# Layer 0's latent columns moved into the context's scan, on one PSUM bank, and the latent scan moved beside the context's selection

## The chip, the cores and the metric

The kernel runs on one core of one Trainium2 chip. The metric is the device time of one execution in microseconds (us). A core has five engines that take their instructions in a fixed order each: TensorE (PE in the profile, its weight loads PEld), VectorE (DVE), ScalarE (ACT), GpSimd (POOL) and SyncE (SP, which here only issues transfers). They wait for each other by semaphores. TensorE writes to PSUM, which holds eight banks of 128 partitions x 512 fp32 numbers.

## The reference

Two layers work on 256 latent tokens `x` and 256 context tokens `z`, 1024 wide; the output is the latents alone. Cut to what matters:

```
def _layer(x, z, c, c_ctx, rows, update_ctx, ...):
    (six modulation vectors of c for x, six of c_ctx for z)
    px = modulate(rmsnorm(x)) @ w_in ;  pz = modulate(rmsnorm(z)) @ w_in
    lat = delta_prep(px) ;  ctx_in = delta_prep(pz)      # conv, SiLU, l2 norm
    oc, sc = gated_delta_chunked(ctx_in, s0=0)           # scan, both directions
    ol, _  = gated_delta_chunked(lat, s0=sc)             # starts from the context's state
    x = x + gate1 * mixer_out(px, ol) @ w_out ;  z likewise   # z only in layer 0
    x = x + gate2 * peer(modulate(rmsnorm(x))) ;  z likewise  # z only in layer 0

def _peer(h, ...):
    scores = (h @ w_query) against sub_keys              # 8 heads, two halves
    idx, gate = top 16 of the pairs of the two halves' top 16
    out = sum_k gate * gelu(h . expert_u[idx]) * expert_v[idx]   # 16384 experts
```

The latents' scan needs the context's scan state, and nothing else of the context. The context's experts (`peer` of `z` in layer 0) need the context's updated `z`, and nothing of the latents.

## The kernel before

The program is written as a list of stages, and a scheduler at build time then decides the order in which each engine's instructions stand; the written order sets its priorities and the order in which shared buffers are handed on. A `Stage` is a piece of SBUF that lives from its opening to its `close()`; a later stage that gets the same addresses waits for the earlier one's last reader. PSUM has names for its eight banks: `pj0`, `pj1`, `c0`, `c1`, `c2`, two of `po`, and one `s`. `bank(shape, tag)` takes the next turn of a name; whoever takes a bank waits until its last user has read it. `using(c0="s", ...)` sends names to other banks for the time of a block: with `c0`, `c1`, `c2` and `pj` all sent to `s`, everything in the block passes through one bank, in the order in which it was written.

The stages of layer 0, by the names used below:

- modulation (L275, vectors 0 to 5 of both token sets): `w_mod` arrives in tiles of 128x1024 (512 KB), four of which fit the ring `w0`, `w1`.
- columns (L404): rmsnorm, transposes into `hT`, then for each part of k, v, q two halves: `columns_by_feature` (16 matmuls 128x128 on 256 columns), copy to `xpad` (L491), convolution on VectorE (L495, L497), SiLU (L500), transposes (L510), for k and q also a norm (L518 to L521) and transposes back (L527). Then `columns_by_token` for the gate `zs` and for the pooling and Fourier heads (L574 to L602).
- scan (L609): four independent chains in the banks `c0`, `c1`, `pj0`, `pj1` (L627 to L680), then steps through `c2`, `c1` into `po` (L704 to L726). Products with the level masks are made on GpSimd (`pool_tt`, L232).
- update (L733): norm of the scan's output, `w_out`, residual.
- select: eight heads of `w_query` and keys on TensorE, top-16 on VectorE. For the context it is `gather_select` (L909), for the latents `dense_select` (L1047) followed by `build` (L1071), which writes a dense gate table to DRAM.
- gather (`gather_rows`, L961): for the context's first 128 tokens `by_choice` fetches 128 rows of `u` and then 128 of `v`, each by one indirect transfer of 512 KB that GpSimd issues (L970) into a ring of seven buffers `uv`. VectorE takes the dot products with u (L982), TensorE sums the v rows (L1005) in bank `s`. For the other 128 tokens `by_token` fetches 128 rows of u and v together.
- stream (L1093): for the latents all 16384 experts, 128 tiles of u and of v; its scores live in bank `s` (L1096), so its first matmul (L1117) waits until `by_choice` has read `s` for the last time (L1010). The gather of `by_token` and layer 1's context run inside it.

Before, the stages are written in this order: context columns, context scan, modulation (2, 4, 3, 5) through `s`, context update, context selection, latent columns, latent scan, latent update, latent selection, build, gather, stream.

Of the kernel before, what the change touches and what calls it, by code (L numbers as in the profile page):

```python
# [24 lines left out]
CTX, LAT = 0, 1  # L25
# [120 lines left out]
def _body(st, tc, a, out, dbg, until):  # L146
# [34 lines left out]
    @contextmanager  # L181
    def using(**kw):
        old = dict(roles)
        roles.update(kw)
        yield
        roles.clear()
        roles.update(old)
# [24 lines left out]
    def dump(key, t):  # L212
        if dbg is not None and key in dbg:
            nc.sync.dma_start(dbg[key], t)

    def to_rows(src, offset, n):
        return bass.AP(tensor=src.tensor, offset=src.offset + offset, ap=[[0, 128], [1, n]])
# [10 lines left out]
    def by_block(name):  # L228
        return [a[name][b * 128 : (b + 1) * 128, :] for b in range(NB)]

    def pool_tt(out, x, y, op):
        pool.tensor_tensor(out, x, y, op=op)  # L232
# [127 lines left out]
    def columns_by_token(name, n, h):  # L360

        ps = [bank([128, 512], "pj") for _ in range(NB)]
        for kh in range(2):
            w = wtile(name, n, kh)
            for kk in range(4):
                k = kh * 4 + kk
                for b in range(NB):
                    product(
                        ps[b], [x[:, b * 128 : b * 128 + 128] for x in h(k)], w(kk, 512), k == 0, k == KT - 1
                    )  # L370
        return ps
# [32 lines left out]
    def columns(l, s, m, full, keep, tl):  # L404
# [139 lines left out]
        if full:  # L544

            zs = keep("zs", [128, NB, 512])
            for b, p in enumerate(columns_by_token(f"wrest{l}", 0, lambda k: [h[:, k] for h in hs])):
                act.activation(zs[:, b], p, AF.Silu)
            dnw = tl("dnw", [128, 128])
            nc.sync.dma_start(dnw, to_rows(a["dnw"], l * 128, 128))  # L550
            pool_tt(
                zs.rearrange("p b (h n) -> p (b h) n", h=4), zs.rearrange("p b (h n) -> p (b h) n", h=4),
                dnw[:, None, :].to_broadcast([128, 8, 128]), op=OP.mult,
            )
            pf = tl("t4", [128, NB, 512], 2)
            for b, p in enumerate(columns_by_token(f"wrest{l}", 1, lambda k: [h[:, k] for h in hs])):
                act.copy(pf[:, b], p)
            mix = tl("hT", [128, KT, T])[:, 0:4] if roles["split"] else keep("mix", [128, 4, T])
            w = T if s == CTX else 128
            for pair in range(2):  # L560
                wpool = tl(f"wpool{pair}", [128, 128])
                nc.sync.dma_start(wpool, a["wpool"][:, l, pair])
                p = bank([128, T], f"c{pair}")
                for gi in range(2):
                    gg = 2 * pair + gi
                    o = slice(gi * 64, gi * 64 + 64)
                    band = tl("band", [128, NB, w], 2)
                    nc.sync.dma_start(band, a[f"band{s}"][:, gg])
                    for b in range(NB):
                        cols = pf[:, b, gg * 64 : gg * 64 + 64]  # L570
                        if s == CTX:
                            pe.matmul(p[o], cols, band[:, b], start=(b == 0), stop=(b == 1))
                        else:
                            pe.matmul(p[o, b * 128 : b * 128 + 128], cols, band[:, b], start=True, stop=True)  # L574
                y = tl("py", [128, T])
                act.copy(y, p)
                p = bank([128, T], f"c{pair}")
                pe.matmul(p, wpool, y, start=True, stop=True)
                dve.tensor_scalar(mix[:, pair], p, psc[:, l, pair : pair + 1], None, op0=OP.mult)
            dft_tok = tl("t4", [128, 2, NB, T], 2)  # L580
            nc.sync.dma_start(dft_tok, a["dft_tok"])
            for pair in range(2):
                wfnet = tl(f"wfnet{pair}", [128, 128])
                nc.sync.dma_start(wfnet, a["wfnet"][:, l, pair])
                fw = tl("fw", [128, 2, 128])
                p = bank([128, 2, 128], f"c{pair}")
                for i in range(2):
                    pe.matmul(p[:, i], dft_ch[:, i], wfnet, start=True, stop=True)
                act.copy(fw, p)
                p = bank([128, 2, T], f"c{pair}")  # L590
                for i in range(2):
                    for b in range(NB):
                        pe.matmul(
                            p[:, i], pf[:, b, 256 + pair * 128 : 256 + pair * 128 + 128], dft_tok[:, i, b],
                            start=(b == 0), stop=(b == 1),
                        )
                fy = tl("fy", [128, 2, T])
                act.copy(fy, p)
                p = bank([128, T], f"c{pair}")
                for i in range(2):  # L600
                    pe.matmul(p, fw[:, i], fy[:, i], start=(i == 0), stop=(i == 1))
                act.copy(mix[:, 2 + pair], p)  # L602
            dump(f"mixb{l}{s}", mix)
            mix = two_parts(mix, *(keep(n, [128, 4, T], 1, F32R) for n in ("mixh", "mixl"))) if roles["split"] else (mix,)
# [304 lines left out]
    def gather_select(l, s, m, rows, done):  # L909
# [6 lines left out]
        h2 = [normed(X[s, b], rows(f"h2{b}", [128, D]), f"n{b}") for b in range(NB)]  # L916
        done()
        sp = Stage("select")
        with using(c0="po", c1="po"):
            hT = transposed(h2, sc, sh, sp("hT", [128, KT, T]))  # L920

        def by_token():
# [234 lines left out]


    m = mods[0]
    sw, ck, cc = Stage("split", "right"), Stage("keep", "right"), Stage("columns", "right")  # L1160
    with using(split=sw, lo="dve"):
        c_state = columns(0, CTX, m, True, ck, cc)
    cc.close()
    for b, src in enumerate(by_block("x")):
        nc.sync.dma_start(X[LAT, b], src)
    cs = Stage("scan", "right")
    c_po = scan(0, CTX, True, c_state, cs)
    cs.close()
    with using(c2="s", pj="s"):
        modulation(0, (2, 4, 3, 5))  # L1170
    cu = Stage("update", "right")
    with using(split=sw, lo="dve"):
        update(0, CTX, m, c_state, c_po, cu)
    cu.close()

    rows = Stage("rows")
    cw = Stage("select_weights")
    with using(c0="s", c1="s", pj="po", ring=cw):
        chosen = gather_select(0, CTX, m, rows, lambda: (ck.close(), sw.close()))
    cw.close()  # L1180

    lk, lc = Stage("keep", "right"), Stage("columns", "right")
    l_state = columns(0, LAT, m, True, lk, lc)
    lc.close()
    ls = Stage("scan", "right")
    l_po = scan(0, LAT, True, l_state, ls)
    ls.close()
# [46 lines left out]
    m = mods[1]  # L1234
    sw, lk, lc = Stage("split", "right"), Stage("keep", "right"), Stage("columns", "right")
    with using(split=sw, lo="dve", c0="po", c1="po", c2="s", sb=1):
        l_state = columns(1, LAT, m, True, lk, lc)
# [14 lines left out]
    sw = Stage("split")  # L1252
# [37 lines left out]
```

## Time and profile before

| | |
|---|---|
| median of 3 runs | 3274.06 us (3268.94 to 3278.41) |
| the profiled execution | 3268.07 us, of which the span shown is 3266.3 us |
| PE busy | 2874.7 us (88%) |
| DVE busy | 2211.1 us (68%) |
| ACT busy | 1349.3 us (41%) |
| POOL busy | 860.3 us (26%) |
| transfers | 746.5 MB, 229 GB/s over the span |

The shares are means over stages with different limits, so the table is only a frame; the prediction reads stage by stage. A stage is found by the lines and names of its instructions. Times of rows are counted from the span's start.

### The profile page before, as it was taken

What the parts mean: (1) busy time and instruction counts of PE and PEld (TensorE: products, weight loads), DVE (VectorE), ACT (ScalarE), POOL (GpSimd) and SP (SyncE); (2) the same over time, 40 slices, a digit from 0 to 9 for tenths busy, and PEclk for the clock granted to TensorE, in tenths of its full rate; (3) what the DMA queues carried; (4) which work ended last, traced back from release to release, by engine and by line L of the source; (5) the groups of instructions that cost most, each with busy time, mean ns of one, the idle gap of its engine ahead of it and who ended that gap; (6) DMA issues with size and microseconds to landing.
All of it is one profiled execution on the core that took longest, in us unless ns stands there. A gap on an engine that the chain in (4) does not pass through costs nothing. (4 is left out here: it accounts for less than half of the span.)

```text
span 3266.3 us, 47152 instructions
## 1 busy us (share of the span) xinstructions
PE 2874.7 (88%) x17467; PEld 2362.5 (72%) x17467; DVE 2211.1 (68%) x4920; ACT 1349.3 (41%) x2352; POOL 860.3 (26%) x638
## 2 busy tenths in 40 slices
PE   7998985779796887887899999999779889999998
PEld 4686845637351776776778999867678778889997
DVE  4534979777880888898885655742599865555555
ACT  4432232101350444444455645542335644544443
POOL 0150148973545333333310123133320000000000
PEclk9998987779999999999899999999889999999999
DMA  7631466697999999999976543361335576666663
GB/s 260 207 103 54 138 244 194 201 330 254 354 373 351 375 369 365 362 395 387 360 278 197 161 140 118 94 221 43 100 123 176 205 237 202 200 210 202 213 212 130
DMA packets 246165, 746.52 MB, mean 229 GB/s; under 512 B 21168, under 2 KB 94256, under 8 KB 225456
## 3 DMA queue, kind: packets, MB, share of 16 engines
q1 hardware_dynamic: 190320, 474.54, 43.3%
q0 software_dynamic: 55296, 268.46, 22.1%
q8 instruction: 137, 2.24, 0.3%
q14 instruction: 92, 0.75, 0.1%
q10 hardware_dynamic: 320, 0.52, 0.1%
HBM read 707.27 MB, written 35.65 MB: 227 GB/s over the span
## 5 line engine op out<-in xcount | busy, mean ns | idle before, releaser
L1117 PE MATMUL s<-Hh,hu 128*128 128x256 f32 x2048 | 605.5, 296 | 75.7 <-ACT hu L1106 53.6
L1119 PE MATMUL s<-Hh,lu 128*128 128x256 f32 x2048 | 603.9, 295 | 55.5 <-DVE lu L1107 55.4
L1118 PE MATMUL s<-Hl,hu 128*128 128x256 f32 x2048 | 596.1, 291 | 0.0
L1117 PEld LDWEIGHTS s<-Hh,hu 128*128 128x128 f32 x2048 | 408.4, 199 | 100.8 <-ACT hu L1106 63.6
L1107 DVE TENSOR_TENSOR lu<-w,hu 128x1024 fp32r<-128x1024 f32 x256 | 317.0, 1238 | 225.4 <-ACT hu L1106 224.7
L1119 PEld LDWEIGHTS s<-Hh,lu 128*128 128x128 f32 x2048 | 408.8, 200 | 68.7 <-DVE lu L1107 68.6
L1107 DVE TENSOR_TENSOR lv<-w,hv 128x1024 fp32r<-128x1024 f32 x256 | 314.4, 1228 | 181.2 <-ACT hv L1106 168.1
L1118 PEld LDWEIGHTS s<-Hl,hu 128*128 128x128 f32 x2048 | 409.0, 200 | 7.8
L1106 ACT CAST hu<-w 128x1024 fp32r<-128x1024 f32 x256 | 267.8, 1046 | 328.3 <-PE s L1118 252.6
L1106 ACT CAST hv<-w 128x1024 fp32r<-128x1024 f32 x256 | 267.4, 1045 | 161.3 <-PE pj L1140 117.8
L970 POOL DMA_INDIRECT uv<-in_uv,idx x128 | 208.4, 1628 | 404.6 <-DVE acc L1029 383.4
L982 DVE SCALAR_TENSOR_TENSOR uv<-uv,h 128x1024 f32<-128x1024 f32 x128 | 193.4, 1528 | 38.7 <-DMA uv<-in_u,idx 37.8
L232 POOL TENSOR_TENSOR C<-L,levels 128x512 f32<-128x512 f32 x96 | 136.8, 1436 | 292.6 <-DMA g<-gd 161.1
L970 POOL DMA_INDIRECT uv<-in_u,idx x128 | 174.5, 1364 | 44.7 <-issue 25.2
L1140 PE MATMUL po<-hv,wh 128*128 128x512 f32 x512 | 164.9, 402 | 13.2 <-ACT wh L1133 12.2
L970 POOL DMA_INDIRECT uv<-in_v,idx_t x128 | 132.3, 1034 | 122.2 <-PE s L1005 95.2
L1140 PE MATMUL po<-lv,wh 128*128 128x512 f32 x512 | 162.4, 398 | 0.6 <-DVE lv L1107 0.5
L1029 DVE SCALAR_TENSOR_TENSOR acc<-uv,dot,acc 128x1024 f32<-128x1024 f32 x127 | 162.6, 1281 | 0.0
L1140 PE MATMUL pj<-hv,wh 128*128 128x512 f32 x512 | 162.5, 397 | 0.0
L1133 ACT CAST wh<-we 128x256 fp32r<-128x256 f32 x256 | 103.4, 404 | 143.0 <-DVE we L1132 78.3
L1088 PEld LDWEIGHTS c<-one,two 128*128 128x128 f32 x1024 | 123.6, 193 | 53.3 <-issue 33.2
L1140 PE MATMUL po<-hv,wl 128*128 128x512 f32 x512 | 161.8, 397 | 0.0
(427 smaller groups left out, 6007.5 us busy)
## 6 DMA issues: line engine op xcount, KB each, us to landing
w<-in_tab SPq DMA_DIRECT2D x512, 512.0 KB, 4.7
w<-in_wmod SPq DMA_DIRECT2D x96, 512.0 KB, 4.8
gd<-gs SPq DMA_DIRECT2D x32, 1024.0 KB, 5.3
g<-gd SPq DMA_DIRECT2D x32, 1024.0 KB, 8.5
w<-in_wq SPq DMA_DIRECT2D x48, 512.0 KB, 4.2
w<-in_win SPq DMA_DIRECT2D x44, 512.0 KB, 4.3
w<-in_wrest SPq DMA_DIRECT2D x24, 512.0 KB, 3.7
w<-in_wout SPq DMA_DIRECT2D x24, 512.0 KB, 5.3
```

The lines of the kernel that those rows point to most:

```text
L232: pool.tensor_tensor(out, x, y, op=op)
L970: pool.indirect_dma_start(out=t, out_offset=None, in_=a[f"{table}{l}"], in_offset=bass.IndirectOffsetOnAxis(ap=index, axis=0))
L982: dve.scalar_tensor_tensor(u, u, 1.0, st["h2", b], op0=OP.mult, op1=OP.mult, accum_out=dots[:, j : j + 1])
L1029: dve.scalar_tensor_tensor(acc, uv[:, D:], dot, acc, op0=OP.mult, op1=OP.add)
L1088: pe.matmul(p[:, t], two[:, t], one[:, t], start=True, stop=True)
L1106: act.copy(hi, raw)
L1107: eng(lo, raw, hi.bitcast(F32), op=OP.subtract)
L1117: pe.matmul(p, hi[:, ks], Hh[:, k], start=(k == 0), stop=False)
L1118: pe.matmul(p, hi[:, ks], Hl[:, k], start=False, stop=False)
L1119: pe.matmul(p, lo[:, ks], Hh[:, k], start=False, stop=(k == KT - 1))
L1133: act.copy(wh, w)
L1140: pe.matmul(acc[b][n], x[:, ts], y[:, n * 512 : n * 512 + 512], start=(i == 0 and j == 0), stop=(i == NKEYS - 1 and j == 2),)
```

## The change

It does five things. The latents' columns are written right after the context's scan, with every bank name sent to `s`. Modulation is cut in two: vector 2 ahead of those columns, vectors 4, 3, 5 behind them. The context's selection sends all its names to `s`, so that the latents' scan, which keeps the other banks, can be taken beside it. The stages are opened in another order, and the three stretches of small weights `wpool0/1`, `wfnet0/1` share one buffer `wpair`. The transposes at the head of `gather_select` go to `c0`, `c1` instead of `po`.

```diff
-                wpool = tl(f"wpool{pair}", [128, 128])
+                wpool = tl("wpair", [128, 128])
...
-                wfnet = tl(f"wfnet{pair}", [128, 128])
+                wfnet = tl("wpair", [128, 128])
...
-        with using(c0="po", c1="po"):
+        with using(c0="c0", c1="c1"):
             hT = transposed(h2, sc, sh, sp("hT", [128, KT, T]))
...
-    sw, ck, cc = Stage("split", "right"), Stage("keep", "right"), Stage("columns", "right")
+    lk, ck, sw, cc = (Stage(n, "right") for n in ("keep", "keep", "split", "columns"))
     with using(split=sw, lo="dve"):
         c_state = columns(0, CTX, m, True, ck, cc)
     cc.close()
+    sw.close()
...
     c_po = scan(0, CTX, True, c_state, cs)
+    with using(c2="s", pj="s"):
+        modulation(0, (2,))
+    lc = Stage("columns")
+    with using(c0="s", c1="s", c2="s", pj="s"):
+        l_state = columns(0, LAT, m, True, lk, lc)
+    lc.close()
     cs.close()
     with using(c2="s", pj="s"):
-        modulation(0, (2, 4, 3, 5))
-    cu = Stage("update", "right")
+        modulation(0, (4, 3, 5))
+    sw, cu = Stage("split", "right"), Stage("update", "right")
     with using(split=sw, lo="dve"):
         update(0, CTX, m, c_state, c_po, cu)
     cu.close()
...
-    with using(c0="s", c1="s", pj="po", ring=cw):
-        chosen = gather_select(0, CTX, m, rows, lambda: (ck.close(), sw.close()))
+    with using(c0="s", c1="s", c2="s", pj="s", ring=cw):
+        chosen = gather_select(0, CTX, m, rows, lambda: (sw.close(), ck.close()))
     cw.close()
 
-    lk, lc = Stage("keep", "right"), Stage("columns", "right")
-    l_state = columns(0, LAT, m, True, lk, lc)
-    lc.close()
     ls = Stage("scan", "right")
```

The scheduler's order shows where that puts the work. On TensorE, at the end of the context's scan, these rows stand before (L726 are the scan's last sums into `po`; L747 and L256 with `dmixh` are the context's update):

```order
L726 MATMUL po_1177<-S_407_1946,qd_358_1758 64x128
L726 MATMUL po_1177<-vn_413_1985,AT_357_1756 64x128
L314 MATMUL c_504_2359<-ident,mod_80 128x128 x4
L747 MATMUL c_479_2235<-ident,ot_475_2213 128x128 x4
L256 MATMUL pj_487_2278<-h_490_2282,dmixh_473_2211 128x512
L256 MATMUL pj_487_2278<-l_491_2283,dmixh_473_2211 128x512
```

and now, at the same place:

```order
L726 MATMUL po_1181<-S_408_1950,qd_359_1762 64x128
L726 MATMUL po_1181<-vn_414_1989,AT_358_1760 64x128
L510 MATMUL s_2287<-ident,y_2277 128x128 x4
L527 MATMUL s_2312<-ident,ktok_2191 128x128 x4
L256 MATMUL s_2323<-hT_2063,w_2319 128x256 x4
L256 MATMUL s_2323<-hT_2063,w_2321 128x256 x4
L256 MATMUL s_2323<-hT_2063,w_2319 128x256 x4
L256 MATMUL s_2323<-hT_2063,w_2321 128x256 x4
L510 MATMUL s_2351<-ident,y_2341 128x128 x4
L256 MATMUL s_2361<-hT_2063,w_2357 128x256 x4
```

Of the latents' columns only the transposes, the gates and the two halves of k's projection stand between the scan's matmuls; the rest of k, all of v and q, the columns by token and the two small heads follow the scan's last row, each in bank `s`. Behind them come the 48 matmuls (L285) of modulation (4, 3, 5), and only then the 96 matmuls of the context's update.

On GpSimd, where the gather has begun, the latents' scan (L232 with `qd`, `S`) stood between the fetches before:

```order
L970 DMA uv_6745<-in_u,idx_2452 128x1024
L970 DMA uv_6748<-in_u,idx_2452 128x1024
L232 TENSOR_TENSOR S_974_4312<-S_1969,dc_3488 128x512
L232 TENSOR_TENSOR S_978_4335<-S_1992,dc_3488 128x512
L970 DMA uv_6751<-in_u,idx_2452 128x1024
L232 TENSOR_TENSOR qd_884_3981<-qd_884_3981,qT_3701 128x512
L970 DMA uv_6754<-in_u,idx_2452 128x1024
```

and now all of it stands ahead of the first fetch, between the selection's own products (`oh`):

```order
L232 TENSOR_TENSOR Q_920_4118<-vtok_2318,fac_2171 128x512
L232 TENSOR_TENSOR oh_3807<-oh_3807,tif_3758 128x1024
L232 TENSOR_TENSOR C_1072_4710<-ktok_2191,fac_2171 128x512
...
L232 TENSOR_TENSOR S_1085_4763<-S_4385,dc_2182 128x512
L232 TENSOR_TENSOR oh_3945<-oh_3945,tif_3915 128x1024
L977 MEMSET wz_6677 128x2048
L970 DMA uv_6680<-in_u,idx_3058 128x1024
L970 DMA uv_6683<-in_u,idx_3058 128x1024
```

On VectorE the 128 dot products with u (L982) stood among the latents' scan and update before, and all of them ahead of the latents' selection. Now the first 16 stand among the update, those from the 17th to the 104th among the selection, and the last 24 among the first 85 of build's 316 instructions. The 128 fetches of v follow the last fetch of u, in both.

On VectorE, at the program's start, the context's norm (L325 to L327) stood ahead of modulation's first result; now it stands behind its third (`mod`, L295), and is mixed with the fourth:

```order
L249 TENSOR_TENSOR l_88_476<-w_473,h_87_475 128x1024
L249 TENSOR_TENSOR l_91_482<-w_479,h_90_481 128x1024
L325 TENSOR_SCALAR ss_233<-ss_233 128x1
L295 TENSOR_REDUCE mod_80<-c_32_187 128x8
L238 TENSOR_SCALAR rst_237<-ss_233 128x1
L299 TENSOR_TENSOR mod_80<-mod_80,bmod 128x16
L239 TENSOR_SCALAR rsy_236<-rst_237 128x1
```

The stage of the context's columns now lies where modulation's first tiles lay, and waits for them.

## Rows read from the trace of the kernel before

**Rows 1.** Page: granted TensorE clock and transfers in 40 slices of 81.7 us.

```profile
PEclk9998987779999999999899999999889999999999
DMA  7631466697999999999976543361335576666663
```

**Rows 2.** Busy time of each engine by stretch, with clock and transfers.

```profile
core 0: us, PE busy (x) PEld busy (x) DVE busy (x) ACT busy (x) POOL busy (x), PEclk, DMA share, GB/s
...
141.00:259.00 118.00, 110.49 (x860) 89.23 (x852) 45.61 (x68) 47.85 (x98) 54.04 (x46) 1.00 0.31 108
259.00:298.00 39.00, 27.70 (x115) 21.67 (x114) 19.81 (x70) 12.61 (x32) 0.20 (x4) 0.87 0.26 78
298.00:442.00 144.00, 132.86 (x632) 109.70 (x633) 120.94 (x647) 39.29 (x95) 18.16 (x10) 0.96 0.38 116
442.00:735.00 293.00, 211.36 (x1013) 150.81 (x1012) 237.79 (x369) 56.00 (x127) 242.14 (x182) 0.77 0.76 257
735.00:850.00 115.00, 96.11 (x508) 64.57 (x510) 94.31 (x541) 20.46 (x40) 47.24 (x37) 0.96 0.79 277
850.00:975.00 125.00, 118.52 (x750) 70.12 (x742) 109.16 (x326) 67.33 (x71) 56.42 (x50) 0.99 0.98 370
975.00:1050.00 75.00, 52.71 (x214) 9.10 (x212) 2.36 (x2) 2.97 (x4) 40.27 (x43) 0.98 1.00 381
1050.00:1620.00 570.00, 471.43 (x2690) 409.77 (x2690) 495.13 (x648) 248.17 (x533) 194.69 (x120) 0.93 0.98 370
1620.00:2040.00 420.00, 410.48 (x2662) 369.95 (x2663) 262.18 (x389) 225.72 (x368) 71.75 (x50) 0.99 0.55 184
```

**Rows 3.** Timeline: the gather's first fetch, its last matmul, the stream's first matmul.

```profile
443.40 1.11 POOL L970 DMA_INDIRECT uv<-in_u,idx  x1 [0.16 <-issue]
```

```profile
1048.86 1.06 PE L1005 MATMUL s<-uv,wz 128*32 128x512 f32 x6 [0.17 <-DMA uv<-in_v,idx_t]
1050.61 0.39 PE L1117 MATMUL s<-Hh,hu 128*128 128x256 f32 x1 [0.69 <-ACT sum L1010]
```

**Rows 4.** Timeline of the start: context's norm, its transposes, first use of the modulation.

```profile
6.27 1.06 ACT L324 ACTIVATE t<-x 128x1024 f32<-128x1024 f32 x1 [2.88 <-DMA x<-in_ctx]
...
12.22 0.69 PE L337 MATMUL c<-ident,t 128*128 128x128 f32 x2
...
44.14 0.99 DVE L343 TENSOR_SCALAR hT<-c,sc,mod 128x256 f32<-128x256 f32 x2
```

**Rows 5.** Groups in 298:485 (latents' columns: pj; context's selection: po): busy, mean.

```profile
L256 PE MATMUL po<-hT,w 128*128 128x256 f32 x256 | 57.6, 379 | 0.0
L256 PE MATMUL pj<-hT,w 128*128 128x256 f32 x192 | 44.1, 381 | 0.0
L256 PE MATMUL pj<-w,hT 128*128 128x512 f32 x64 | 30.2, 627 | 0.0
L497 DVE SCALAR_TENSOR_TENSOR y<-xpad,convw,y 128x256 f32<-128x256 f32 x36 | 15.9, 478 | 0.0
L500 ACT ACTIVATE y<-y 128x512 f32<-128x512 f32 x6 | 3.8, 630 | 26.6 <-DVE y L497 26.6
L491 ACT COPY xpad<-pj 128x512 f32<-128x512 f32 x6 | 3.5, 584 | 3.1 <-PE pj L256 3.1
```

**Rows 6.** Modulation in 100:190: its matmuls (groups), its tiles' transfers (DMA view).

```profile
L285 PE MATMUL s<-w,cvec 128*32 128x512 f32 x128 | 20.4, 601 | 0.0
```

```profile
w<-in_wmod SPq DMA_DIRECT2D x31, 512.0 KB, 4.6
```

**Rows 7.** Line 982, the dot products with u: durations in ns, and their waits.

```profile
L982 DVE SCALAR_TENSOR_TENSOR uv<-uv,h x128: 1210/1225/3918, 447.8 to 730.7; 128x1024 f32<-128x1024 f32 x128
...
  DMA uv<-in_u,idx: 37.8, 41
```

**Rows 8.** Timeline: such a product beside a GpSimd product of the latents' scan.

```profile
603.04 2.82 DVE L982 SCALAR_TENSOR_TENSOR uv<-uv,h 128x1024 f32<-128x1024 f32 x1 [1.17 <-DMA uv<-in_u,idx]
603.72 1.04 POOL L232 TENSOR_TENSOR L<-ktok,fac 128x512 f32<-128x512 f32 x1
```

## Prediction

> **What bounds the kernel now.** I read the slices of the page first, then the stages one by one as stretches, then the timeline at the borders between stages. The slices [rows 1] show that no engine bounds the whole: transfers stand at 9 tenths from about 820 to 1630 us, are under 5 tenths between 160 and 410 us, and the granted clock dips to 7 between 490 and 740 us. The stretches [rows 2] give each stage its limit. The context's scan (141 to 259 us) is TensorE's: 110.5 of 118 us busy. The context's selection (298 to 442 us) is VectorE's, 120.9 of 144 us, with TensorE at 132.9. From 442 to 735 us the 128 products with u run beside the latents' scan; VectorE is busy for 237.8 of 293 us and the transfers stand at 0.76. Then come the latents' selection (735 to 850, VectorE 94.3 us) and build (850 to 975, VectorE 109.2 us, transfers 0.98), and until 1050 us nearly nothing but fetches of v: transfers 1.00, VectorE 2.4 of 75 us. From 1050 to 1620 us the stream shares the transfers (0.98) with the second gather, and from there TensorE is busy for 410 of 420 us.
>
> The border at 1050 us matters most. The last matmul of the first gather ends at 1049.9 us, and the stream's first matmul starts at 1050.6 [rows 3], since both use bank `s`. Behind that border there is no slack: first the transfers and then TensorE are full, and the order behind it is practically the old one. So I take a shift of this border as a shift of the end. The border is the gather's start (first fetch at 443.4 us [rows 3]) plus the gather's length, 607 us now. Both change.
>
> **The gather's start.** It needs the context's selection, which needs the context's update, which needs the context's scan. The latents' columns were beside the selection; now most of them stand ahead of the update on TensorE.
>
> - Head: the context's norm now follows the third result of modulation. Before, Square started at 6.3 us, the transposes at 12.2 us and the first use of the modulation at 44.1 us [rows 4], so the norm's 6 us and the first transposes were covered by modulation. Without that cover they cost about 8 us.
> - Context's scan: TensorE is the limit. The columns' part that stands in it is two of six k/v/q groups at 44.1 / 6 = 7.35 us [rows 5], and some 12 us of transposes and gate matmuls (an estimate): 27 us. Three quarters of modulation leave it, of 20.4 us of matmuls and some 5 of transposes [rows 6]: -19. That is +8 us. The shared buffer `wpair` is filled only after its last reader, three times behind one another; a tile of 512 KB lands in 4.6 us [rows 6], these are an eighth of it; between 0 and 4.6 us each, I take 2: +6 us.
> - Rest of the columns, on one bank: a group's matmuls (7.35 us), its copy (0.58), eight convolution instructions of 0.48 (3.8), SiLU (0.63) [rows 5], transposes (0.6) and copy (0.6) must follow one another, because the bank's next turn is written behind the last reader of this one. That is 13.5 us for each of two groups of v. For each of two of q a norm (squares, twelve short VectorE instructions, product, about 5) and a second pair of transposes and copy (1.2) come on top: 19.5 us. k's second half still owes 6 us. The columns by token are four turns of 30.2 / 4 = 7.55 us [rows 5] and a copy, 33 us. The two heads are eight short turns, about 15 us, with some 3 us for `wpair`, and 4 us of table loads. Sum: 27 + 39 + 6 + 33 + 18 + 4 = 127 us; of these TensorE works some 75, and with gaps of 5 us and more its clock should lie between the 0.77 and the 0.98 of the less busy stretches [rows 2], for which I add 6: 133 us. Below it can't go under the 75 us of matmuls. Nothing else can use TensorE meanwhile but the 8 transposes of the update.
> - Modulation (4, 3, 5), which was hidden in the scan: six halves of four tiles, through a ring of four. Its matmuls and transposes alone are 6/8 of 25 us, 19; four tiles of 4.6 us landing time [rows 6] that start as the last half frees them give some 7 to 9 us for a half. I take 42 us, between 19 and 55.
> - Update: 39 us before from the scan's end to the selection's start (259 to 298, [rows 2]); its norm and transposes are now hidden beside the columns: -6 us.
> - Selection: 145 us before, from 298 to 443. The latents' scan takes the columns' place. On TensorE the selection has 57.6 us of projections [rows 5] and some 14 of keys and transposes, the scan about 100 (from 110.5 in the context's stretch, less the modulation in it), of which two thirds stand ahead of the last head's scores: 140 us, at 95% 148. The norm ahead costs 8 us, the last head's top-16 on VectorE some 17 behind. 173 us: +28.
>
> Start: 8 + 8 + 6 + 133 + 42 - 6 + 28 = +219 us, that is about 662 us.
>
> **The gather's length.** The latents' scan leaves it, and with it a blockade: a product with u takes 1.225 us in the median but up to 3.9 [rows 7], and the long ones stand beside the scan's GpSimd products, as the 2.8 us at 603 us [rows 8]. In exchange the latents' selection now lies beside u. Up to the last u VectorE has 128 x 1.3 = 167 us, the selection's 94 (735 to 850), some 10 of the update, and 85 of build's 316 instructions, 0.27 x 109 = 29 [rows 2]: 300 us. Before, it was busy for 81% of such a stretch, with 37.8 us of waits for transfers [rows 7]; the transfers now have more time for each u, so I take 91%: 330 us (300 to 370). Then v: 67 MB, twelve of build's sixteen writes of 1.05 MB, and 5 MB of the stream's first tiles, at the 381 GB/s of the last stretch [rows 2], is 223 us. With 7 us of borders that is 560 us: -47.
>
> **Sum.** 219 - 47 = +172 us. The profiled execution took 3268.07 us, 1.8 more than its span and 6 less than the median of the runs. 3268 + 172 = 3440; I say 3438.
>
> Here a rule of the Trainium skill bears on the largest term. The Trainium skill (Perfetto Trace Analysis, Optimizing Tensor Performance, Matmuls) has independent groups rotate through different PSUM banks, so that the evacuation of one overlaps the matmuls of the next. Read by itself it would price the one bank at its evacuations, 0.6 us each, some 14 us on 75 of matmuls, and the sum would be +128 us. The rows say more: between two turns of the bank lie the convolution, SiLU and the norm, not only a copy.
>
> **The rivals.**
>
> - The one bank costs little. If TensorE is fed throughout, the columns' rest is 75 to 87 us and modulation about 25. For it: the stretches with most matmuls are over 90% busy [rows 2]; the written order may be loosened by the scheduler. Against it: the rows in the order stand one turn behind the other. +172 - 50 - 17 = +105 us: 3373. Chance 0.18.
> - TensorE at its lower clock. The granted clock is 0.77 in the mean from 442 to 735, where TensorE has gaps [rows 2], and its levels are 1.2 and 2.4 GHz. If the columns' rest and modulation run at the lower one, their 95 us of matmuls double; 30 of the extra lie under modulation's transfers: +172 - 6 + 65 = +231 us: 3499. Against it: 975 to 1050 had gaps too, at 0.98. The Trainium skill (TensorE: Matmul & The Clock Gate, Part 1) has the lower clock as the default after idleness; by this rule the rest would run so, and the rows bear it out in part. Chance 0.20.
> - Faster: the gather without the scan becomes bound by transfers alone. 134 MB of u and v and some 38 MB of weights, build's writes and tiles at 381 GB/s are 452 us, 155 less than now. With the columns fed as in the first rival, modulation at 19, the scan for nothing in the selection and no price at the head, the start shifts by 8 + 75 + 19 - 6 = +96: 3209. It decides where the gather shrinks by more than its start moves. Against it: VectorE's 300 us up to the last u cannot lie beside v's 67 MB, since v's fetches stand behind u's. Chance 0.04.
> - The change doesn't show: the stream takes the delay up. For it: nothing but transfers at 0.98 that could be better spread. Against it: both its halves are full. 3274, chance 0.04.
> - The forecast, 0.54.
>
> **Numbers.** The range takes in the first two rivals and the bounds of the gather's length: 3345 to 3530, with a tenth on each side outside. About 0.3% is what a measurement of this kernel can tell from no change. Faster by more than that has the 0.04 of its rival and 0.01 for the unforeseen; same 0.04; slower 0.91.
>
> **What would show it.** The context's scan ends at about 281 us (last L726 into `po`), the columns' last matmul (L601) at about 414, modulation's last transposes at 456, the update's last matmul near 483, the first fetch (L970) at about 662. The median of L982 stays at 1.22 us and its mean falls from 1.53 to about 1.3. The stream's first L1117 comes at about 1222 us and the stream is as long as before. Between 281 and 456 TensorE shows gaps of several us ahead of L510 and L256, ended by ACT and DVE, and transfers stay low. The prediction is wrong if the first fetch comes before 560 us, or if fewer than 500 us lie between it and the stream's first matmul, or if the stream gets shorter.

## The result, and the profile after

The changed kernel takes 3425.03 us (3422.68 to 3431.59, 4 runs) against 3276.23 us (3268.94 to 3283.85, 4 runs) for the kernel before: ratio 1.0456, 95% interval 1.0432 to 1.048. It is slower by 149 us. The forecast was 3438 us, in a range of 3345 to 3530; the forecast case holds, and its largest term, the one bank, came out to within one microsecond in its sum, though not in its parts. Other terms were mis-sized, and partly cancel.

The page of the changed kernel, TensorE's granted clock and the transfers in 40 slices of 85.7 us:

```profile
PEclk8898889988579999999989999999988999999999
DMA  6301252099789989999998554244133666666663
```

Against [rows 1], the hollow of the transfers is longer: from the second slice to the eighth (86 to 686 us) no digit is above 5. The first gather starts only then. Busy times by stretch in the changed kernel, to be laid beside [rows 2]; the stretches are the context's scan, the rest of the latents' columns, modulation (4, 3, 5), the context's update, its selection to the last scores, the rest of it, the u part and the v part of the first gather, and two of the stream:

```profile
core 0: us, PE busy (x) PEld busy (x) DVE busy (x) ACT busy (x) POOL busy (x), PEclk, DMA share, GB/s
...
177.00:289.00 112.00, 111.26 (x808) 93.18 (x807) 39.98 (x78) 38.11 (x75) 44.56 (x39) 1.00 0.06 20
289.00:423.00 134.00, 88.54 (x285) 56.97 (x284) 25.87 (x103) 19.83 (x66) 2.34 (x1) 0.81 0.22 70
423.00:465.00 42.00, 26.59 (x121) 6.04 (x120) 1.71 (x10) 3.88 (x7) 0.00 (x0) 0.92 0.87 300
465.00:492.00 27.00, 25.01 (x104) 20.11 (x104) 12.71 (x15) 9.24 (x10) 0.00 (x0) 0.94 0.59 195
492.00:640.50 148.50, 134.09 (x886) 124.07 (x886) 120.05 (x523) 53.81 (x117) 61.72 (x47) 0.95 0.19 58
640.50:683.50 43.00, 41.40 (x280) 29.80 (x280) 24.36 (x90) 4.09 (x8) 10.85 (x9) 1.00 0.00 1
683.50:988.00 304.50, 159.10 (x654) 111.63 (x654) 288.52 (x918) 48.02 (x83) 188.65 (x143) 0.73 0.88 319
988.00:1207.00 219.00, 177.93 (x889) 64.46 (x889) 81.04 (x240) 49.24 (x52) 120.31 (x122) 0.97 0.97 373
1207.00:1780.00 573.00, 458.06 (x2676) 398.48 (x2676) 488.95 (x642) 243.86 (x525) 194.50 (x119) 0.93 0.96 366
1780.00:2200.00 420.00, 407.71 (x2644) 365.61 (x2645) 262.74 (x392) 228.85 (x372) 64.84 (x49) 0.99 0.55 187
```

From 289 to 465 us there is a hole that the kernel before does not have: 176 us in which TensorE has 115 us of work, VectorE 28 and ScalarE 24. In the columns' rest (289 to 423 us) nearly all of the idle time is waits between two turns of the one bank; in modulation behind it (423 to 465) TensorE is idle for 15 us, 9.3 of them for tiles of `w_mod`. What TensorE waited for in the columns' rest, by its chain of waits (engine, line, releaser: us in total, times, longest):

```profile
PE s L510 <- ACT y L500: 17.8, 4, 4.5
PE s L527 <- DVE fy L521: 8.9, 2, 4.5
PE s L527 <- DVE ktok L521: 5.0, 1, 5.0
PE s L574 <- DMA band<-in_band: 2.7, 1, 2.7
PE s L588 <- DMA wpair<-in_wfnet: 2.0, 1, 2.0
```

The first three rows are the convolution with SiLU, and the norm: 31.7 of some 45 us of waits. The copies out of the bank, a row of 0.5 to 1.4 us each below these, are the smaller part.

The borders on which the prediction stood, by the timeline: the first fetch, the first gather's last matmuls and the stream's first matmul (beside [rows 3]).

```profile
683.55 1.11 POOL L970 DMA_INDIRECT uv<-in_u,idx  x1 [0.16 <-issue]
```

```profile
1205.32 1.06 PE L1005 MATMUL s<-uv,wz 128*32 128x512 f32 x6 [0.20 <-DMA uv<-in_v,idx_t]
1207.08 0.39 PE L1117 MATMUL s<-Hh,hu 128*128 128x256 f32 x1 [0.69 <-ACT sum L1010]
```

The first fetch is 240 us later (443.4 to 683.5), the gather 84 us shorter (607 to 524), the stream's start 156 us later, and the stream with all behind it 7 us longer (2222.6 against 2215.7 us). The two parts of the gather, u and v, in the kernel before, to be laid beside the stretches 683.50:988.00 and 988.00:1207.00 above:

```profile
443.40:732.00 288.60, 206.96 (x1004) 148.85 (x1003) 236.13 (x367) 55.73 (x127) 239.24 (x180) 0.77 0.76 256
732.00:1050.60 318.60, 270.34 (x1473) 145.12 (x1471) 206.13 (x869) 91.59 (x115) 145.59 (x132) 0.97 0.91 339
```

At 339 GB/s for 318.6 us the v part before moved 108 MB, at 373 GB/s for 219 us it now moves 82; the u part went from 74 to 97 MB. The program's start, beside [rows 4]: the context's norm is now where the first use of the modulation was.

```profile
43.71 1.06 ACT L324 ACTIVATE t<-x 128x1024 f32<-128x1024 f32 x1
...
48.45 0.66 PE L337 MATMUL c<-ident,t 128*128 128x128 f32 x2 [3.93 <-DVE rsy L243]
...
50.74 1.19 DVE L343 TENSOR_SCALAR hT<-c,sc,mod 128x256 f32<-128x256 f32 x2 [1.00 <-PE c L337]
```

Modulation's matmuls in 423 to 465 us (beside [rows 6]; the trace has two rows for each of the 48), and the products with u (beside [rows 7]):

```profile
L285 PE MATMUL s<-w,cvec 128*32 128x512 f32 x96 | 22.5, 671 | 10.8 <-DMA w<-in_wmod 9.3 <-DVE mod L295 0.8 <-ACT mix L602 0.5
```

```profile
L982 DVE SCALAR_TENSOR_TENSOR uv<-uv,h x128: 1158/1218/5630, 688.0 to 986.5; 128x1024 f32<-128x1024 f32 x128
...
  DMA uv<-in_u,idx: 11.3, 11
```

### The profile page after: what moved, and what is told of

Read it like the earlier page. It is cut to its first block, busy times and chain, and to the rows that moved or that the text cites. A ratio compares the mean times of both kernels' runs of the same rounds, so it can differ in the third digit from the quotient of the medians.

```text
span 3429.7 us, 47104 instructions
## 1 busy us (share of the span) xinstructions
PE 2892.9 (84%) x17467; PEld 2359.3 (69%) x17467; DVE 2189.9 (64%) x4920; ACT 1341.6 (39%) x2344; POOL 834.5 (24%) x638
## 5 line engine op out<-in xcount | busy, mean ns | idle before, releaser
L1119 PE MATMUL s<-Hh,lu 128*128 128x256 f32 x2048 | 596.9, 291 | 53.5 <-DVE lu L1107 53.5
L232 POOL TENSOR_TENSOR C<-L,levels 128x512 f32<-128x512 f32 x96 | 128.5, 1351 | 318.8 <-DVE L L645 180.6
L970 POOL DMA_INDIRECT uv<-in_u,idx x128 | 159.9, 1249 | 106.3 <-DVE uv L982 49.3
L1088 PEld LDWEIGHTS c<-one,two 128*128 128x128 f32 x1024 | 137.1, 211 | 68.5 <-issue 50.0
L1088 PE MATMUL c<-one,two 128*128 128x128 f32 x1024 | 150.5, 303 | 37.8 <-DVE one L1087 36.7
L982 DVE SCALAR_TENSOR_TENSOR uv<-uv,h 128x1024 f32<-128x1024 f32 x128 | 159.3, 1268 | 11.3 <-DMA uv<-in_u,idx 11.3
L1089 ACT COPY gs<-c 128x512 f32<-128x512 f32 x128 | 128.4, 1057 | 92.6 <-PE c L1088 86.9
```

The lines of the kernel that those rows point to most:

```text
L970: pool.indirect_dma_start(out=t, out_offset=None, in_=a[f"{table}{l}"], in_offset=bass.IndirectOffsetOnAxis(ap=index, axis=0))
L982: dve.scalar_tensor_tensor(u, u, 1.0, st["h2", b], op0=OP.mult, op1=OP.mult, accum_out=dots[:, j : j + 1])
L1088: pe.matmul(p[:, t], two[:, t], one[:, t], start=True, stop=True)
L1089: act.copy(gs[:, :, t4 : t4 + 4].rearrange("p i t -> p t i"), p)
L1119: pe.matmul(p, lo[:, ks], Hh[:, k], start=False, stop=(k == KT - 1))
```

## The experiments

Times are medians beside runs of the kernel before on the same chip; each ratio is to those. The spans are of the one profiled execution, which lies up to 12 us from the median (e1). The borders that the text compares, read from the traces in us (end of the context's scan, last matmul of the latents' columns, end of modulation, end of the context's update, first fetch, last product with u, first matmul of the stream, span):

| kernel | scan | columns | mod. | update | fetch | last u | stream | span |
|---|---|---|---|---|---|---|---|---|
| before | 259.3 | 486.0 | 191.9 | 291.9 | 443.4 | 731.9 | 1050.6 | 3266.3 |
| changed | 289.1 | 423.1 | 464.8 | 492.1 | 683.5 | 987.8 | 1207.1 | 3429.7 |
| e1_free_banks | 296.6 | 380.9 | 391.7 | 418.7 | 609.9 | 913.3 | 1138.0 | 3352.1 |
| e2_mod_in_scan | 288.2 | 455.8 | 190.3 | 441.0 | 628.6 | 932.9 | 1158.8 | 3384.6 |
| e3_select_only | 262.3 | 470.2 | 195.8 | 295.0 | 492.6 | 793.8 | 1066.7 | 3284.8 |
| e4_columns_only | 289.6 | 424.0 | 464.9 | 490.4 | 647.2 | 953.2 | 1183.8 | 3400.6 |
| e5_both | 294.5 | 384.7 | 189.0 | 403.8 | 588.3 | 891.5 | 1116.9 | 3345.7 |
| e6_scan_on_vector | 259.9 | 487.8 | 193.0 | 293.0 | 445.0 | 686.6 | 1037.5 | 3257.6 |
| e7_columns_free | 295.3 | 386.2 | 189.9 | 406.7 | 561.4 | 862.7 | 1092.2 | 3313.7 |
| e8_two_buffers | 280.8 | 417.9 | 459.7 | 487.2 | 665.3 | 973.0 | 1197.9 | 3417.1 |
| e9_onehot_on_vector | 259.2 | 485.1 | 191.3 | 291.5 | 442.7 | 736.8 | 1056.4 | 3273.5 |
| e10_both_on_vector | 259.3 | 485.5 | 191.6 | 291.6 | 443.0 | 680.9 | 1024.2 | 3235.2 |
| e11_after_on_vector | 287.5 | 422.9 | 463.6 | 491.3 | 671.1 | 953.3 | 1181.4 | 3394.8 |
| e12_gather_first | 260.2 | 487.9 | 193.1 | 293.3 | 445.1 | 683.4 | 1007.7 | 3256.9 |

**e1: the columns' rest on free banks.**

```diff
         by_token(1, ktok, kT, 1.0)
+        if l == 0 and s == LAT:
+            for name in ("c0", "c1", "c2", "pj"):
+                roles.pop(name)
```

> The changed kernel, but of the latents' columns only the head, the gates and k pass through bank s; v, q, the columns by token and the two small heads take the banks c0, c1, c2, pj0 and pj1 again, still behind the context's scan. Theory of the one bank: in the changed kernel 132 us lie between the scan's last sums and the columns' last matmul, of which TensorE works 87; it waits 32 us for SiLU and the norm (L500, L521), and the granted clock is 0.81. With free banks these waits vanish and the clock rises above 0.9: the rest of the columns takes 90 to 102 us, and the time is 3425 - 30 to 42 = 3383 to 3395 us. Rival, the place is what costs and not the bank (TensorE's work and the small transfers): 120 us or more, and 3412 to 3428 us.

Measured: 3366.12 us, ratio 1.0274 (1.0235 to 1.0312). The theory's sign holds, but it went too short: the columns' rest takes 84 us, not 90 to 102, and the gain is 59 us, not 30 to 42. The stretches of this kernel, the columns' rest and then what is left of modulation:

```profile
297.00:381.00 84.00, 77.91 (x335) 43.01 (x336) 23.16 (x89) 18.45 (x59) 2.35 (x1) 1.00 0.62 202
381.00:392.00 11.00, 7.25 (x32) 2.12 (x28) 0.98 (x4) 2.15 (x5) 0.00 (x0) 0.93 1.00 384
```

The columns' rest falls from 134 to 84 us at full clock, and inside it lie 78 of modulation's 96 rows, since `s` is now free for them: only 11 us of modulation are left behind. TensorE's waits for SiLU and the norm are gone; what it waits for in these 84 us is this, and 0.3 us more:

```profile
PE s L285 <- DMA w<-in_wmod: 5.3, 7, 1.7
```

So the one bank cost 50 us in the columns and 31 in modulation; the scan, which takes in more of the columns, gives 7 of these 81 back, and the first fetch comes 74 us earlier. I had left the second price out.

**e2: all of modulation in the context's scan again.**

```diff
-        modulation(0, (2,))
+        modulation(0, (2, 4, 3, 5))
...
-    with using(c2="s", pj="s"):
-        modulation(0, (4, 3, 5))
```

> The changed kernel, but all of modulation (2, 4, 3, 5) is written ahead of the latents' columns, so that it lies in the context's scan again. Theory of the lost cover: the 41 us of modulation behind the columns vanish; its 19 us of TensorE lengthen the scan, from which some 8 us of the columns' work move out, and the update can start inside the columns' gaps, which hides 10 to 25 us of its 29: the gather's first fetch 30 to 47 us earlier, the time 3378 to 3395 us. Rival, the chain through bank s only moves: modulation's 41 us on s delay the columns by as much as they save, first fetch within 10 us of the changed kernel, 3415 to 3430 us.

Measured: 3385.16 us, ratio 1.0323 (1.0282 to 1.0364), first fetch 55 us earlier. The theory's time holds, but the fetch moved by more than its 30 to 47 us. Modulation costs the scan nothing (288.2 against 289.1 us): in exchange half of k's projections moves out of it. The columns end 33 us later, because their chain on `s` starts later (its first transposes at 193 us instead of 168), as the rival had it in part. What gains is that the update no longer stands behind the columns' last turn: it ends 15 us before they do.

**e3: the selection's part of the change alone, on the kernel before.**

```diff
-        with using(c0="po", c1="po"):
+        with using(c0="c0", c1="c1"):
...
-    with using(c0="s", c1="s", pj="po", ring=cw):
+    with using(c0="s", c1="s", c2="s", pj="s", ring=cw):
```

> The kernel before, with one part of the change alone: the context's selection passes through bank s (transposes at its head through c0, c1); columns, modulation and stages stay as they were. Theory that the selection is limited by VectorE and the one bank costs it little: its scores wait for at most two copies of 0.6 us per head, 0 to 10 us in all; first fetch at 443 to 455 us, the latents' scan still inside the gather, the gather 595 to 610 us, the time 3266 to 3290 us. Rival, the one bank in the selection is itself a large part of the 40 us by which the selection grew: first fetch at 465 us or later, 3295 us or more.

Measured: 3285.89 us, ratio 1.0025 (1.0009 to 1.0042). The time is the theory's, the reason is not: the first fetch came at 492.6 us, as the rival said, 49 us later. From the first to the last scores the kernel before and this one read:

```profile
318.00:411.00 93.00, 91.16 (x472) 80.65 (x471) 84.17 (x489) 25.17 (x60) 10.84 (x6) 1.00 0.44 135
```

```profile
319.00:461.00 142.00, 141.11 (x676) 110.93 (x675) 102.81 (x564) 41.25 (x99) 13.82 (x7) 1.00 0.44 131
```

TensorE is full in both. On one bank the selection's next projection stands behind the reader of the last one, so more of its neighbour's matmuls are put ahead of it: 204 more in the stretch, nearly all of them the latents' columns. TensorE doesn't wait; the selection gives it away. Most of it comes back: the v part of the gather takes 273 us instead of 319, with the latents' work done earlier.

**e4: the columns' part alone; the selection has its banks of before** (the line of e3 the other way round, and its transposes on `po`).

> The changed kernel without the selection's part: the selection has its banks of before (s for c0 and c1, po for its projections and transposes), so that the latents' scan, whose sums need po, falls behind it in part. Theory that the latents' scan pays in the selection what it saves in the gather: first fetch 10 to 25 us earlier than the 683 us of the changed kernel, L982's mean back above 1.30 us, the gather 535 to 560 us instead of 524, the time 3410 to 3435 us. Rival, the scan beside the selection is a gain by itself: first fetch where it was, gather longer by 30 us or more, 3445 us or more.

Measured: 3408.46 us, ratio 1.0406 (1.0367 to 1.0446). First fetch 36 us earlier, gather 537 us (13 longer), L982's mean 1.281 us against 1.268. The time is just below the theory's, and the mean did not go back above 1.30. The gain at the fetch is more than the 10 to 25 us expected: from update to fetch 157 us instead of 191 (152 before). The 34 us are not the bank's alone. With `po` in the selection, part of the latents' scan falls behind it: of its 800 matmul rows (L617 to L726) 257 come after the first fetch, against 6 in the changed kernel, and 343 instead of 533 stand ahead of the selection's last scores. This run does not tell the price of the bank from that of the scan's work which the bank lets in.

**e5: e1 and e2 together.**

> The changed kernel with both edits that gained: v, q, the columns by token and the heads on free banks, and all of modulation in the context's scan. With free banks alone, modulation already ended 11 us behind the columns, because bank s was free for it; so little of its 42 us is left to gain. Theory that TensorE's work between scan and update is what remains: the update starts when the columns end, first fetch 590 to 602 us (610 with free banks alone), gather 525 to 533, time 3346 to 3360 us. Rival, the two gains of 73 and 55 us at the first fetch add up because they have different causes: first fetch below 575 us, time below 3335 us.

Measured: 3341.25 us, ratio 1.0183 (1.016 to 1.0207); first fetch 588.3 us. Time and fetch lie just below the theory's ranges and well above the rival's 575 us at the fetch: the two gains overlap in part (95 us at the fetch together, 74 and 55 apart), and what is left between scan and update, 109 us, is mostly TensorE's work (e7's rows show the like).

**e7: the changed kernel's order with the banks freed** (e5 with e4's selection). The columns' transposes, gates and k still pass through `s`, but inside the context's scan.

> The stages in the changed kernel's order, but with no stage on one bank: free banks for the columns, all of modulation in the scan, and the selection's banks of before. Theory that the single banks cost the time and the order itself little: selection 157 us instead of 191, first fetch at 553 to 570 us, gather 535 to 545, stream from 1090 to 1113, time 3308 to 3332 us, still slower than before, since some 85 us of TensorE's work on the columns stand ahead of the update and the gather gives back only 65. Rival, the latents' scan out of the gather pays for all that: 3277 us or less.

Measured: 3315.34 us, ratio 1.011 (1.0085 to 1.0135). Time and fetch are as the theory said: the first fetch 118 us later than before, the gather 76 us shorter, 531 us and so 4 below its range. This order loses about 35 us; the single banks, with modulation's place behind one, about 110. As in e4, 257 of the latents' scan's 800 rows lie beside the gather here, so the order is not wholly the changed kernel's. This kernel from scan to update, in two stretches:

```profile
295.00:386.00 91.00, 80.60 (x317) 55.89 (x318) 33.12 (x114) 23.75 (x71) 2.35 (x1) 0.91 0.39 127
386.00:407.00 21.00, 20.16 (x96) 16.01 (x95) 8.95 (x11) 5.74 (x7) 0.00 (x0) 1.00 0.43 150
```

**e8: two buffers for the small weights** (`wp0` for the first pair, `wp1` for the second, in place of `wpair`).

> The changed kernel with two buffers in turn for the four small weights instead of one. Theory of the shared buffer: in the changed kernel TensorE waits 5.07 us for wfnet (L588) before the context's scan and 2 to 3 us in the latents' columns; with two buffers the context's last L627 into bank c comes 5 to 7 us earlier (154 before) and the first fetch 5 to 10 us earlier (683 us), the time 3415 to 3421 us. Rival, hidden by the scan's other waits: first fetch within 2 us, 3423 to 3428 us.

Measured: 3420.24 us (two runs), ratio 1.0428 (1.0398 to 1.0458), which the intervals do not tell apart from the changed kernel. In the trace the context's last L627 into `c` stands at 145.2 us instead of 153.7 and the scan ends 8 us earlier; the columns' rest is 137 us. The first fetch is 18 us earlier, more than the buffer explains, and half of that is gone at the stream's start. The few microseconds of the buffer are real at the border, unproven in the time.

**e6: on the kernel before, the latents' scan's 46 products on VectorE.**

```diff
+        tt = dve.tensor_tensor if (l, s) == (0, LAT) else pool_tt
...
-                pool_tt(qd, qd, qT[:, :, b * 128 : b * 128 + 128], op=OP.mult)
+                tt(qd, qd, qT[:, :, b * 128 : b * 128 + 128], op=OP.mult)
...
```

> The kernel before, with one edit: the elementwise products of the latents' scan (46 of them) are done on VectorE instead of GpSimd. Theory that the long products with u come from GpSimd's work beside them: the mean of L982 falls from 1.53 to 1.30 us or less, 29 to 36 us over 128; VectorE takes 46 products of 0.69 us in exchange, 32 us, so the gather stays at 595 to 612 us and the time at 3262 to 3290 us. Rival, the long ones come from the transfers that write the ring at the same time: the mean of L982 stays above 1.45 us, the gather grows by the products' 20 to 32 us, the time 3290 us or more.

Measured: 3252.25 us, ratio 0.9907 (0.9881 to 0.9933): faster, and 10 us below the theory's span. The products with u in this kernel (the line is 983 here), beside [rows 7]:

```profile
L983 DVE SCALAR_TENSOR_TENSOR uv<-uv,h x128: 1207/1216/1246, 449.3 to 685.4; 128x1024 f32<-128x1024 f32 x128
...
  DMA uv<-in_u,idx: 16.8, 17
```

The longest falls from 3.918 to 1.246 us, the mean to 1.217, and u takes 47 us less (288.5, now 241.6). Of this 32 us are lost again on v, 351 us instead of 319. So the long products do come from GpSimd's elementwise work, and something else holds v.

**e9 and e10: the latents' one-hot products on VectorE, alone and with e6.** In the kernel before GpSimd waits in the v part for these things (fetches are issued on GpSimd, in its fixed order):

```profile
POOL uv L970 <- PE s L1005: 95.2, 47, 6.2
POOL oh L232 <- DVE oh L857: 31.4, 5, 13.2
...
POOL oh L232 <- DVE start L845: 10.6, 1, 10.6
```

```diff
+        lat = l == 0 and tuple(groups) == (HEADS,)
...
-            pool_tt(oh, oh, tif[:, :, :, None].to_broadcast(shape), op=OP.mult)
+            (dve.tensor_tensor if lat else pool_tt)(oh, oh, tif[:, :, :, None].to_broadcast(shape), op=OP.mult)
```

> The kernel before, with one edit: in the latents' selection of layer 0 the eight products with the one-hot table (oh) are done on VectorE instead of GpSimd. Theory of GpSimd's queue: in the kernel before GpSimd stands 43 us before these products, for VectorE, with the fetches of v queued behind them; without them the part of the gather behind the last u falls from 319 to 285 to 300 us, and the time by 15 to 30 us, to 3248 to 3263 us. Rival, TensorE's order holds the ring anyway (GpSimd also waits 95 us for L1005): that wait grows by as much, the part stays above 310 us, 3270 to 3282 us.

> The kernel before with both edits: the latents' scan's products and the latents' one-hot products of layer 0 on VectorE. Theory that the two act on different parts of the gather (the products with u; the fetches of v) and add up: u 237 us, v 315 to 330 instead of 351, gather 557 to 575, time 3222 to 3242 us. Rival, behind a faster u the fetches of v wait for TensorE, which has the update and the selection in front: v stays at 345 us or more, 3248 us or more.

Measured: e9 3269.41 us, ratio 0.9969 (0.9946 to 0.9992); e10 3244.19 us, ratio 0.9897 (0.9865 to 0.9928). In e9 the theory falls: v takes 320 us as before, and the wait has only moved, in the same stretch of this kernel:

```profile
POOL uv L971 <- PE s L1006: 152.4, 51, 28.2
```

The ring's buffers come free when TensorE has summed the v rows, and those matmuls stand behind the latents' update and selection. With both edits (e10) v is 343 us and the time 3244, both between the two forecasts.

**e11: both edits on the changed kernel.**

> The changed kernel with the same two edits. Theory that the change shortened the gather by taking these very products out of the way (none of the scan's and only one wait of 5 us for the one-hot products are left in it): they bring little more here, the gather 515 to 530 us instead of 524; in the selection VectorE gets some 30 us of products on top of its 144 of 191, first fetch 683 to 700 us; time 3418 to 3445 us. Rival, GpSimd's products cost the changed kernel as well: gather below 505 us, 3405 us or less.

Measured: 3398.34 us, ratio 1.036 (1.0329 to 1.0391), which is the rival's time, though the gather did not fall below its 505 us. The first fetch is 12 us earlier and the gather 13 us shorter, 510 us. I had counted the products only as a load on VectorE; GpSimd takes 1.0 to 1.4 us in the mean for a product of the scan that VectorE does in 0.69, and in the changed kernel they lie on the selection's and the scan's chains.

**e12: e10 with the gather written ahead of the latents' update, selection and build.**

```diff
+    fetching = gather_rows(0, CTX, m, rows, chosen)
+    for _ in range(EARLY):
+        next(fetching)
     lu = Stage("update", "right")
     update(0, LAT, m, l_state, l_po, lu)
...
-    fetching = gather_rows(0, CTX, m, rows, chosen)
-    for _ in range(EARLY):
-        next(fetching)
```

> The kernel before with both edits on VectorE, and the gather written ahead of the latents' update, selection and build instead of behind them. In TensorE's order 75 rows of other work then stand among the first quarter of the v matmuls, instead of 212. Theory that the fetches of v were held by TensorE's order (GpSimd waits 174 us for L1007 with both edits, and the transfers are at 0.83, 0.66 and 0.86 from 681 to 860 us, some 40 us of idle transfers): v 300 to 320 us instead of 343, gather 540 to 560 us, time 3204 to 3226 us. Rival, the selection and build come later by as much, so that the stream's first tiles of u and build's writes lie behind v: v 340 us or more or the stream longer by 20 us, 3235 us or more.

Measured: 3253.39 us, ratio 0.9913 (0.9896 to 0.9929). v falls from 343 to 324 us, so the order did hold 19 us of it; but the stream and all behind it take 2249 us instead of 2211, so the rival decides. What in the stream grows stays open.

## Why the prediction was right

The terms of the sum, by the same borders, in us:

| step | predicted | measured | read from |
|---|---|---|---|
| head | +8 | +6 | first L627 into `pj`: 119.5, now 125.5 |
| `wpair` | +6 | +6 | last L627 into `c`: 141.4, now 153.7, less the head |
| context's scan | +8 | +18 | the rest of 259.3 to 289.1 |
| columns' rest | +133 | +134 | 289.1 to 423.1 |
| modulation (4, 3, 5) | +42 | +42 | 423.1 to 464.8 |
| update | -6 | -5 | 27.3 us instead of 32.6 |
| selection | +28 | +40 | 191.4 us instead of 151.5 |
| first fetch | +219 | +240 | 443.4, now 683.5 |
| gather | -47 | -84 | 607, now 524 |
| stream | 0 | +7 | 2215.7, now 2222.6 |

- **The one bank** was rightly priced as a chain, not as copies. The Trainium skill (Perfetto Trace Analysis, Optimizing Tensor Performance, Matmuls) has independent groups rotate through banks; e1 agrees, and puts the price at 81 us with modulation's part (74 at the first fetch), where evacuations alone would have been some 14 by the prediction's estimate. Its parts were off: TensorE works 88 us in the rest where I had 75 and 6 more for its clock, and waits 45 where I had 52. The rival "one bank costs little" is refuted by e1. The rival of the lower clock holds for a share only: the granted clock was 0.81 in the columns' rest and 0.92 in modulation, where its price of 59 us needed the lower level throughout.
- **The scan** was mis-sized by 10 us: some 3 before its first L617, where ScalarE now does the latents' norm (two L324) and a table of the gates ahead of L634, the rest inside it, where TensorE is busy for 111 of 112 us. What came in was priced rightly: TensorE is busy in bank `s` for 27.7 us of 161.4 to 289.1, where I had 27. The step that failed is what leaves: I took 19 us of modulation out of the scan, but behind its first L617 (146.4 us) the kernel before had only 13.0 us of it (L285 10.2, L293 2.8); the rest lay ahead of the scan.
- **The selection** was mis-sized by 12 us, and by one part of it. To its last scores it takes 148 us where I had 156, with 533 of the scan's 800 matmul rows ahead of them: two thirds, as I had. Behind them I had 17 us of top-16; it took 43, in the kernel before already 33 (the 32.4 us behind 411 us). (These two miss by 18 us and not by 12, because I counted the selection before from 298 us and the table counts it from the update's last matmul at 291.9.) In the changed kernel VectorE, in its fixed order, waits there for steps of the latents' scan, by its waits from 640 to 684 us:

```profile
DVE vn L706 <- PE c L704: 10.6, 6, 5.9
DVE S L716 <- PE c L710: 4.6, 2, 2.4
```

  I had put the term down to the scan's work. e4, where the selection falls by 34 us, does not refute that, since with the bank a third of the scan's rows leave too.
- **The gather** was mis-sized by 37 us: u with its border 304 us where I had 330 and 7, since VectorE had 289 us of work there instead of 300 and was busy for 95% of the time instead of 91%; v 219 where I had 223, as priced by its bytes. The reason that I gave ahead of the numbers was not the one that counts here. The products did get shorter (mean 1.53 to 1.27 us), but u as a whole got 16 us longer, because the latents' selection lies beside it now; v got 100 us shorter. The larger part of that is transfers: 26 MB less cross in the v part (108, now 82 MB), which at its 373 GB/s are 70 us by my estimate; mostly weights of the latents' selection and `w_mod` tiles, which now land beside u. That the selection no longer stands ahead of the v sums on TensorE is the likely rest: e12, which puts the v sums ahead of the update, the selection and build, gains 19 us of v by it, but no run gives its share in the changed kernel. e6 shows the shorter products by themselves.
- **The stream** took up nothing, so the shift came through. Its 7 us are within what single executions of these kernels spread, 2211 to 2229 us without e12.

The two larger errors, +21 at the start and -37 in the gather, cancelled to 16 us; that the time came out 13 us from the forecast is in this part luck. Of the loss, the single banks, with modulation behind one, make some 110 us and the order some 35 (e7).

## What to carry to other kernels

Price a bank that is shared by a whole stage by everything that must run between two of its turns, and then by who else needs the bank: here modulation behind the columns cost a further 31 us. A stage on one bank that shares TensorE loses its place in the order as well: more of its neighbour's matmuls go ahead of it, with no idle time on TensorE to show it. Before moving a stage out of the way of a gather, ask which of its instructions disturb the gather; moving 46 products from GpSimd to VectorE made the kernel some 30 us faster (e6), where moving the stage lost 149 us.

## What was not expected of the hardware

Next to GpSimd's elementwise products, a VectorE product of two operands in SBUF took up to 3.9 us; with the products away the longest of 128 was 1.246 us, though GpSimd still issued all its fetches beside them (e6). The changed kernel has a longer one yet, the 5.63 us above, and it is beside a single GpSimd operation of the latents' selection:

```profile
759.69 4.78 POOL L232 TENSOR_TENSOR Hl<-hT,Hh 128x2048 fp32r<-128x2048 f32 x1
...
759.92 5.63 DVE L982 SCALAR_TENSOR_TENSOR uv<-uv,h 128x1024 f32<-128x1024 f32 x1
```

The product ends at 765.55 us, 1.1 us behind that operation, nearly the 1.22 us that it takes alone. The Trainium skill (SBUF — State Buffer, SBUF: two separate sides) says that the second port pair is locked between VectorE, when it has two SBUF inputs, and a GpSimd operation that reads SBUF, for the whole instruction. These rows agree; that the issue of a fetch is not such an operation is how e6 reads.
